# Spilled attention outputs kept as one fp32 piece in three device tensors, and a place of its own for each token tile's probabilities

## The chip, the cores and the metric

The kernel runs on one core of one Trainium2 chip. The metric is the device time of one execution in microseconds (us); lower is better. Each kernel is timed in several runs and its median counts. One execution of each was also taken by the hardware profiler, which records when each instruction ran, what it waited for and what the DMA queues moved. Engines are called as in the profile: PE is TensorE's multiplier, PEld its loading of weights, DVE is VectorE, ACT is ScalarE, POOL is GpSimd, SP is SyncE, which here only issues DMAs. L12 is line 12 of the kernel.

## What is computed

One decoder layer in fp32 for 512 tokens of width 2048: RMSNorm, an attention mixer with sixteen heads in four groups, a residual add, RMSNorm, a SwiGLU feed-forward block of width 5632, and a last RMSNorm. The mixer has three branches: compressed keys, selected blocks and a sliding window, each with its softmax and its gate. Cut to what matters here:

```python
proj = h @ w_in
q, kc, vc, ks, vs, kw, vw, gl = jnp.split(proj, bounds, axis=-1)
...
p_c = masked_softmax(s_c, mask_c)
o_c = jnp.einsum('bghtc,bcgd->btghd', p_c.astype(vcc.dtype), vcc)
...
o = (gates[:, :, 0, :, :, None] * o_c + gates[:, :, 1, :, :, None] * o_s
     + gates[:, :, 2, :, :, None] * o_w)
return o.reshape(Bsz, S, N_HEADS * DH) @ w_out
```

With 512 tokens every block is selected and the window reaches back over all tokens, so both large branches are causal attention, with keys and values of their own.

## The kernel before, in words

**Numbers.** Every fp32 operand of a product is kept as two fp32r parts, a high one (an ACT copy) and a low one (a DVE subtraction of that copy from the operand). `three` (L267 to L269) multiplies high by high, high by low and low by high, so each product is three matrix multiplications. A weight granule is loaded by DMA into a `raw` tile (L81), split by ACT into `whi` (L97) and by DVE into `wlo` (L98); `take` and `ahead` keep the loads and splits some granules ahead of use. In the attention stage `W.queue` is POOL's queue, elsewhere SP's.

**The attention stage** (L630 to L900) issues all instructions in an order written out by hand, with two interleaved streams. No engine reorders its own instructions.

The first stream is the heads. For head h and token tile t (128 tokens each):

- `scores` (L769) multiplies queries by keys into PSUM (`s`), adds the bias on DVE (L791) and takes the exponential on ACT (L793) into `P[t]`. For the three branches the widths differ with t, so `P[t]` has 4 x 96, 160, 224 or 288 columns for t of 0 to 3.
- `finish` (L796) scales by gate and sum (L798 to L805), transposes in blocks of 32 x 32 on DVE (L806) and stores `P[t]` with four DMAs on SP to `d_p` (L808).
- `fetch` (L810) brings `d_p` back on SP, rearranged, into `PT` (`ptr`, L812).
- `turn` (L819) splits one piece of `PT` into `pth` (ACT, L829) and `ptl` (DVE, L833); for the compressed branch the low part lies in spare rows of `pth` (L831). There are three `pth` and two `ptl`.
- `values` (L836) multiplies the values by it into PSUM (`o`; the compressed branch is L844).
- `head_out` (L849) takes the head's output away.

Only two tiles hold probabilities: `P[0]` and `P[2]` share one, `P[1]` and `P[3]` the other.

A head takes twelve steps. In step i the loop does `turn` number i (nine of them), `values` number i - 2 (so the last in step 10, with `head_out`), and `scores` of the next head in steps 2, 5, 8 and 11 with its `finish` in steps 3, 6, 9 and the next head's step 0. The returns of tiles 1 and 0 are issued in steps 0 and 3, those of tiles 3 and 2 for the next head in step 8.

The second stream, `dense`, fills PE between these steps: projections of queries, keys and values for later heads (`qpair`, `kpair`, `vpair`), and at the end four times `partial`, which multiplies the outputs of heads 0 to 11 by a quarter's columns of the output projection and adds the residual. `pump` closes each step: it runs pieces of `dense` until a goal is reached that grows by 20800 units a head up to 13 heads and by 18300 after. A piece counts 650 units and has three multiplications 512 wide in the projections of queries and keys, and six multiplications 256 wide in `vpair` and `partial`. The whole stream has 13 x 20800 + 4 x 15600 = 332800 units. What is left at the end is run after the last head (`drain_to(100)`).

**The spill.** The normalized input lies in `hn_h` and `hn_l` (16 chunks of 128 rows) until the last projection, `qpair(14)`, has used it; `partial` and the stage after it want the heads' outputs in the same place. So for heads 0 to 11 `head_out` splits the output into two parts and stores both to `d_o` on SP; for heads 12 to 15 it splits straight into `hn_h` and `hn_l`. In `qpair(14)`, after each of its first three granules, `reload_o` brings four heads back with two DMAs of 1 MB on SP.

`partial` loads the residual into a `stage` tile on SP (L702), adds the products (L717) and stores the sum to `d_h` on SP (L718). There is one `stage` tile.

Of the kernel before, what the change touches and what calls it, by code (L numbers as in the profile page):

```python
# [10 lines left out]
F32 = mybir.dt.float32  # L11
F32R = mybir.dt.float32r  # L12
I32 = mybir.dt.int32
AF = mybir.ActivationFunctionType
OP = mybir.AluOpType
# [4 lines left out]
S, D, H, DH, G, HPG = 512, 2048, 16, 128, 4, 4  # L20
NT, KC = S // 128, D // 128
# [152 lines left out]
def nsa_block(ctx: ExitStack, tc: tile.TileContext, x, rel_bias, mix_g, ffn_g, fin_g, w_in, w_out,  # L174
              pos_k, w1k, w2k, pos_v, w1v, w2v, f_in, f_out, onehot, out):
    nc = tc.nc
    mm, act, dve, pool = nc.tensor.matmul, nc.scalar.activation, nc.vector, nc.gpsimd
# [6 lines left out]
    dram = ctx.enter_context(tc.tile_pool(name="dram", bufs=1, space=DRAM))  # L184
# [10 lines left out]
    hn_h, hn_l = hn_t = [hnp.tile([128, KC, S], F32R, name=f"hn_{x}") for x in "hl"]  # L195
    d_t = dram.tile([H, UL], F32, name="d_t")
    d_u = dram.tile([128, H * UL], F32, name="d_u")
    d_c = dram.tile([H, 16 * CL], F32, name="d_c")
    d_o = dram.tile([12, 2, 128, S], F32, name="d_o")
    d_h = dram.tile([S, 256 * N_SPILL], F32, name="d_h")  # L200
    d_r = dram.tile([NT, 128, D], F32, name="d_r")
    d_a = dram.tile([NF // 2, 128, 2 * S], F32, name="d_a")
# [87 lines left out]
    def split_from(psum_ap, hi, lo, scale=None):  # L290
        if scale is None:
            act(hi, psum_ap, AF.Copy)
            dve.tensor_tensor(lo, psum_ap, hi.bitcast(F32), op=OP.subtract)
        else:
            act(hi, psum_ap, AF.Copy, scale=scale)
            dve.scalar_tensor_tensor(lo, psum_ap, scale, hi.bitcast(F32), op0=OP.mult, op1=OP.subtract)
# [53 lines left out]
    with ExitStack() as st1:  # L350
# [11 lines left out]
        with ExitStack() as st0:  # L362
# [79 lines left out]
            p = bank([128, 512])  # L442
            for i in range(N_WARM):
                nc.tensor.transpose(p[:, 128 * (i % 4):128 * (i % 4 + 1)], ident, ident)
            p = bank([128, KC])
# [10 lines left out]
            for q in range(4):  # L456
# [22 lines left out]
                if q == 3:  # L479
                    p = bank([128, S])  # L480
# [100 lines left out]
        for i in range(8):  # L581
# [10 lines left out]
            if i == 1:  # L592
                p = ps1.tile([128, 128], F32, name="tr")
# [27 lines left out]
        p = ps1.tile([96, G, 128], F32, name="tr")  # L621
# [8 lines left out]
    with ExitStack() as st2:  # L630
        ap_ = st2.enter_context(tc.tile_pool(name="ap", bufs=2))
        ps2 = st2.enter_context(tc.tile_pool(name="ps2", bufs=2, space=PSUM))
        kv_tiles(ap_, 1, bufs=1)
        runs = [32 * (2 * t + 3) for t in range(NT)]
        two = [ap_.tile([128, 4 * runs[t]], F32, name=f"p{t}", bufs=1) for t in (2, 3)]
        P = [two[t % 2][:, :4 * runs[t]].rearrange("p (j r) -> p j r", j=4) for t in range(NT)]
        CX = [ap_.tile([128, 32], F32, name=f"cx{t}", bufs=1) for t in range(NT)]
        PT = ap_.tile([128, 4, PT_STEP * 3 + runs[3]], F32, name="ptr", bufs=1)
        d_p = [dram.tile([4, 32, 4, runs[t]], F32, name=f"d_p{t}") for t in range(NT)]
        for t in range(2):  # L640
            pool.memset(two[t], 0.0)
        for t in range(NT):
            pool.memset(CX[t], 0.0)
        done = {"n": 0, "ns": 0}

        def stage_tile():
            return ap_.tile([128, 1024], F32, name="stage", bufs=1)
# [7 lines left out]
        def qpair(h0):  # L655
            ps = proj2()
            end = q_out(ps, h0)
            for i in range(4):
                yield from ws(ps, i, W.take(), end=end)
                if h0 == H - 2 and i < 3:  # L660
                    reload_o(i)
            done["n"] += 1
            yield None

# [27 lines left out]
            yield None  # L692

        def reload_o(i):
            for part, t in enumerate((hn_h, hn_l)):
                nc.sync.dma_start(t[:, 4 * i:4 * i + 4].bitcast(F32),
                                  d_o[4 * i:4 * i + 4, part].rearrange("h p s -> p h s"))

        def partial(cb):
            st = stage_tile().rearrange("p (t c) -> p t c", t=NT)  # L700
            c = slice(256 * cb, 256 * (cb + 1))
            nc.sync.dma_start(st, x[:, c].rearrange("(t p) c -> p t c", p=128))  # L702
            ps = [p.rearrange("p (t c) -> p t c", t=2) for p in proj2()]
            for i in range(3):
                w = W.take()
                for t in range(NT):
                    if i == 2 and t == 2:
                        W.ahead(3)
                    for k in range(4):
                        h = 4 * i + k  # L710
                        three(ps[t // 2][:, t % 2], hn_h[:, h, tok(t)], hn_l[:, h, tok(t)], w[0][:, k], w[1][:, k],
                              h == 0 and t % 2 == 0, h == 11)
                        if k % 2:
                            yield 650
                    if i == 2 and t % 2:
                        b = t // 2
                        dve.tensor_tensor(st[:, 2 * b:2 * b + 2], st[:, 2 * b:2 * b + 2], ps[b], op=OP.add)  # L717
            nc.sync.dma_start(d_h[:, c].rearrange("(t p) c -> p t c", p=128), st)  # L718
            done["n"] += 1
            yield None  # L720

# [13 lines left out]

        def pump(h, step):
            at = h + (step + 4) / STEPS
            goal = 20800 * min(at, 13) + 18300 * max(at - 13, 0)
            while done["ns"] < goal:
                c = next(stream, "end")  # L740
                if c == "end":
                    return
                done["ns"] += c or 0
# [66 lines left out]
        def fetch(t):  # L810

            nc.sync.dma_start(PT[:, :, PT_STEP * t:PT_STEP * t + runs[t]], d_p[t].rearrange("j a i r -> (j a) i r"))  # L812
# [6 lines left out]
        def turn(h, b, kt):  # L819
            n = S - 128 * kt  # L820
            th = ap_.tile([128, 512], F32R, name="pth", bufs=3)
            tl = ap_.tile([128, 512], F32R, name="ptl")
            rows = 128 if b >= 0 else 96
            if b < 0:
                src = arrived(rows, 64, 0, PT_STEP + 64)
            else:
                src = arrived(rows, PT_STEP * kt + 32 * (kt + 1) * b + 32 * kt, kt, PT_STEP + 32 * b)
            th4, tl4 = (x[:rows, :n].rearrange("p (t i s) -> p t i s", i=4, s=32) for x in (th, tl))
            act(th4, src, AF.Copy)  # L829
            if b < 0:  # L830
                dve.tensor_tensor(th4[32:64], src[32:64], th4[32:64].bitcast(F32), op=OP.subtract)  # L831
            else:
                dve.tensor_tensor(tl4, src, th4.bitcast(F32), op=OP.subtract)  # L833
            HS[h]["t", b, kt] = th[:rows, :n], tl[:rows, :n]

        def values(h, b, kt):  # L836
            s, g = HS[h], h // HPG
            first = "o" not in s
            if first:
                s["o"] = ps2.tile([128, 512], F32, name="o", bufs=1)  # L840
            th, tl = s.pop(("t", b, kt))
            o = s["o"][:, 128 * kt:]
            if b < 0:
                mm(o, vcc[:, g], th, start=first, stop=True, skip_group_check=True)  # L844
            else:
                vh, vl = (v[:, kt, 128 * b:128 * (b + 1)] for v in VV[g % 2])
                three(o, vh, vl, th, tl, first, False)

        def head_out(h):  # L849
            o = HS[h]["o"]  # L850
            if h < 12:
                f = [ap_.tile([128, S], F32R, name=f"of{i}", bufs=1) for i in range(2)]
                split_from(o, *f)
                for i in range(2):
                    nc.sync.dma_start(d_o[h, i], f[i].bitcast(F32))
            else:
                split_from(o, hn_h[:, h], hn_l[:, h])
            del HS[h]
# [3 lines left out]
        load_bias(1)  # L862
        for i in range(4):
            scores(0, 3 - i)
            if i:
                finish(0, 4 - i)
            if i > 1:
                fetch(5 - i)
            pump(-1, min(9 + i, 11.7))
        for h in range(H):  # L870
            seq = [(b, kt) for kt in (3, 2, 1, 0) for b in (0, 1)] + [(-1, 0)]
            for i in range(STEPS):
                if i == 4:
                    load_bias(h + 2)
                if i in (0, 3):
                    fetch(1 - i // 3)
                if i < 9:
                    turn(h, *seq[i])
                if i == 8 and h + 1 < H:
                    fetch(3)  # L880
                    fetch(2)
                if i == 0:
                    finish(h, 0)
                if h + 1 < H:
                    if i == 2:
                        drain_to(needed(h + 1))
                    if i % 3 == 2:
                        scores(h + 1, 3 - i // 3)
                    elif i % 3 == 0 and i:
                        finish(h + 1, 4 - i // 3)  # L890
                if 2 <= i < 11:
                    if i == 2 and h % HPG == 0:
                        drain_to(h)
                    values(h, *seq[i - 2])
                    if i == 10:
                        head_out(h)
                pump(h, i)
        W.queue = nc.sync
# [78 lines left out]
    hn_h, hn_l = n2_hl  # L977
# [512 lines left out]
```

## Time and profile before

| | us |
|---|---|
| median of 3 runs | 2137.48 |
| lowest and highest | 2137.11 and 2138.2 |
| the profiled execution | 2137.68 |
| its span, first to last instruction | 2136.0 |
| PE busy in the span | 2103.2 |
| DVE, ACT, POOL busy | 1634.8, 922.9, 118.2 |

The span is some 1.7 us shorter than the time of the profiled execution. In a row by stretches stand the stretch, its length, and then for each engine the time busy and the number of instructions in parentheses; at its end stand the granted TensorE clock as a share of full speed, the share of time that the DMA engines were busy, and GB/s. A row of a timeline has the start, the duration, engine, line, operation and tiles; brackets hold the idle time of that engine just before, and what ended it. A row of waits has the waiting engine and line, what it waited for, the total, how often, and the longest. In a group of instructions stand the busy time and the mean duration in ns.

### The profile page before, as it was taken

To read this page: it belongs to the slowest core of one execution; us is meant where nothing else is said; L and a number is where in the kernel's file an instruction comes from. 1 tells how busy PE (TensorE), PEld (TensorE's weight loads), DVE (VectorE), ACT (ScalarE), POOL (GpSimd) and SP (SyncE) were. 2 spreads that over 40 slices of the span, in tenths; PEclk is the share of its full clock that TensorE was granted. 3 is DMA by queue.
4 is the path that set the end of the run, shared out by engine and by line. 5 is a ranking of instruction groups with operands and counts; after the bars stand their busy time and mean duration, and the time that the engine had idled before them with its cause. 6 is when DMAs were issued, how large, how long until landed. Compare 5 with 4: busy or idle time off the path is not lost.

```text
span 2136.0 us, 37198 instructions
## 1 busy us (share of the span) xinstructions
PE 2103.2 (98%) x14697; PEld 1949.5 (91%) x14697; DVE 1634.8 (77%) x2680; ACT 922.9 (43%) x1433; POOL 118.2 (6%) x195
## 2 busy tenths in 40 slices
PE   9999999999998999999999999999999999999998
PEld 7898788898988889899999999999999888999996
DVE  5565777878776357898888888888888787877785
ACT  5344454555544234444444343443434444544344
POOL 1000111111100000000000000000000000001000
PEclk9999999999999999999999999999999999999999
DMA  7555777776787643344434344433344776878894
GB/s 226 174 158 149 195 203 202 194 209 197 207 295 211 218 137 111 118 130 128 129 126 122 122 126 129 129 119 125 123 129 129 256 278 220 299 268 308 307 336 143
DMA packets 279147, 394.37 MB, mean 185 GB/s; under 512 B 34763, under 2 KB 208891, under 8 KB 278332
## 3 DMA queue, kind: packets, MB, share of 16 engines
q1 hardware_dynamic: 255324, 289.68, 43.5%
q0 software_dynamic: 21744, 98.12, 13.3%
q10 hardware_dynamic: 1904, 4.20, 0.5%
q8 instruction: 115, 1.88, 0.4%
q14 instruction: 60, 0.49, 0.1%
HBM read 323.67 MB, written 73.50 MB: 186 GB/s over the span
## 4 chain that ended last, share of the span: by engine, by line
PE 87%; DVE 5%; DMA 4%; ACT 2%; issue 2%; SPq 1%; POOL 0%; ACTq 0%; DVEq 0%; POOLq 0%
PE f L268 19%; PE f L269 19%; PE f L267 19%; PE proj L267 7%; PE proj L268 6%; PE proj L269 6%; DMA d_p<-p 1%; DVE wlo L98 1%; DMA ptr<-d_p 1%; PE pp L269 1%; PE pp L268 1%; PE pp L267 1%; PE po L269 1%; PE po L267 1%; PE po L268 1%
## 5 line engine op out<-in xcount | busy, mean ns | idle before, releaser
L98 DVE TENSOR_TENSOR wlo<-raw,whi 128x1024 fp32r<-128x1024 f32 (+1 forms) x226 | 270.6, 1200 | 117.2 <-ACT whi L97 116.7
L97 ACT ACTIVATE whi<-raw 128x1024 fp32r<-128x1024 f32 (+1 forms) x226 | 234.4, 1040 | 230.4 <-DVE raw L989 124.7
L989 DVE TENSOR_TENSOR tlo<-tt,thi 128x1536 fp32r<-128x1536 f32 (+2 forms) x135 | 197.1, 1460 | 110.1 <-ACT thi L1091 89.1
L267 PE MATMUL f<-hn_h,whi 128*128 128x256 f32 x984 | 271.7, 276 | 0.8 <-ACT E L1049 0.8
L269 PE MATMUL f<-hn_h,wlo 128*128 128x256 f32 x984 | 271.6, 276 | 0.0
L268 PE MATMUL f<-hn_l,whi 128*128 128x256 f32 x984 | 271.6, 276 | 0.0
L1086 ACT ACTIVATE whi<-raw 128x1024 fp32r<-128x1024 f32 x123 | 126.1, 1057 | 292.2 <-DVE raw L989 281.9
L267 PE MATMUL proj<-hn_h,whi 128*128 128x512 f32 x512 | 204.1, 399 | 0.5 <-ACT hn_h L402 0.5
L268 PE MATMUL proj<-hn_l,whi 128*128 128x512 f32 x512 | 200.7, 392 | 0.3 <-DVE hn_l L403 0.3
L269 PE MATMUL proj<-hn_h,wlo 128*128 128x512 f32 x512 | 200.9, 392 | 0.0
L267 PEld LDWEIGHTS f<-hn_h,whi 128*128 128x128 f32 x984 | 184.7, 188 | 1.2 <-ACT E L1049 1.2
L269 PEld LDWEIGHTS f<-hn_h,wlo 128*128 128x128 f32 x984 | 184.7, 188 | 0.0
L268 PEld LDWEIGHTS f<-hn_l,whi 128*128 128x128 f32 x984 | 184.7, 188 | 0.0
L1091 ACT ACTIVATE thi<-tt 128x1536 fp32r<-128x1536 f32 x82 | 121.8, 1486 | 84.8 <-PE f L268 75.3
L989 DVE TENSOR_TENSOR wlo<-raw,whi 128x1024 fp32r<-128x1024 f32 x123 | 147.0, 1223 | 0.0
L267 PE MATMUL proj<-whi,hn_h 128*128 128x256 f32 (+2 forms) x496 | 146.7, 296 | 0.0
L269 PE MATMUL proj<-whi,hn_l 128*128 128x256 f32 (+2 forms) x496 | 146.0, 294 | 0.0
L268 PE MATMUL proj<-wlo,hn_h 128*128 128x256 f32 (+2 forms) x496 | 145.9, 294 | 0.0
L269 PE MATMUL f<-whi,tlo 128*128 128x512 f32 x320 | 124.9, 390 | 0.6 <-DVE tlo L989 0.6
L268 PE MATMUL f<-wlo,thi 128*128 128x512 f32 x320 | 125.0, 391 | 0.0
L267 PE MATMUL f<-whi,thi 128*128 128x512 f32 x320 | 124.7, 390 | 0.0
L269 PEld LDWEIGHTS proj<-hn_h,wlo 128*128 128x128 f32 x512 | 96.5, 189 | 21.5 <-DVE wlo L98 0.2
(323 smaller groups left out, 6087.1 us busy)
## 6 DMA issues: line engine op xcount, KB each, us to landing
raw<-in_ffn_w_in SPq DMA_DIRECT2D x135, 512.0 KB, 3.8
raw<-in_ffn_w_out SPq DMA_DIRECT2D x88, 512.0 KB, 5.7
rawx<-in_ffn_w_in SPq DMA_DIRECT2D x41, 512.0 KB, 4.8
rawx<-d_a SPq DMA_DIRECT2D x31, 512.0 KB, 5.2
ah<-d_s POOLq DMA_DIRECT2D x16, 896.0 KB, 7.0
al<-d_s POOLq DMA_DIRECT2D x16, 896.0 KB, 9.5
raw<-in_nsa_w_in SPq DMA_DIRECT2D x24, 512.0 KB, 5.1
raw<-in_nsa_w_in POOLq DMA_DIRECT2D x24, 512.0 KB, 4.7
```

The source lines that it names most:

```text
L97: self.nc.scalar.activation(hi[:, :n], src, AF.Copy)
L98: self.nc.vector.tensor_tensor(lo[:, :n], src, hi[:, :n].bitcast(F32), op=OP.subtract)
L267: mm(o, ah, bh, start=start, stop=False, skip_group_check=True)
L268: mm(o, ah, bl, start=False, stop=False, skip_group_check=True)
L269: mm(o, al, bh, start=False, stop=stop, skip_group_check=True)
L989: dve.tensor_tensor(o, a, b, op=OP.subtract)
L1086: act(h, r, AF.Copy)
L1091: act(h, ttf, AF.Copy)
```

## The change

- `d_o` becomes three tensors of four heads, with one fp32 piece for each head instead of two parts.
- `head_out` of heads 0 to 11 copies the output by ACT into the `stage` tile and stores that, with one DMA.
- `reload_o` brings four heads back into `hn_l` alone, with one DMA of 1 MB on POOL's queue.
- A new `split_o` splits two heads in place: ACT copies from `hn_l` to `hn_h`, DVE subtracts. Two such splits are issued in `qpair(14)`, after its third and its last granule, and four in the first `partial`, ahead of the pieces of tiles 0 and 2 of its granules 0 and 1.
- `partial` loads `stage` and stores to `d_h` on POOL's queue, and the load comes after its second granule is taken.
- `P[t]` has a tile for each t; POOL clears all four, largest first.
- Before head 0 the return `fetch` goes ahead of the next tile's `finish`.
- The goal of `pump` grows by 22500 units a head after 13 heads, not by 18300.
- `turn` of the compressed branch takes no `ptl` tile.
- The last of the nine `values`, and `head_out`, move from step 10 to step 11.

```diff
-    d_o = dram.tile([12, 2, 128, S], F32, name="d_o")
+    d_o = [dram.tile([4, 128, S], F32, name=f"d_o{i}") for i in range(3)]
...
-        two = [ap_.tile([128, 4 * runs[t]], F32, name=f"p{t}", bufs=1) for t in (2, 3)]
-        P = [two[t % 2][:, :4 * runs[t]].rearrange("p (j r) -> p j r", j=4) for t in range(NT)]
+        P = [ap_.tile([128, 4, runs[t]], F32, name=f"p{t}", bufs=1) for t in range(NT)]
...
-        for t in range(2):
-            pool.memset(two[t], 0.0)
-        for t in range(NT):
+        for t in reversed(range(NT)):
             pool.memset(CX[t], 0.0)
+            pool.memset(P[t], 0.0)
...
                 yield from ws(ps, i, W.take(), end=end)
                 if h0 == H - 2 and i < 3:
                     reload_o(i)
+                if h0 == H - 2 and i > 1:
+                    split_o(i - 2)
...
         def reload_o(i):
-            for part, t in enumerate((hn_h, hn_l)):
-                nc.sync.dma_start(t[:, 4 * i:4 * i + 4].bitcast(F32),
-                                  d_o[4 * i:4 * i + 4, part].rearrange("h p s -> p h s"))
+            pool.dma_start(hn_l[:, 4 * i:4 * i + 4].bitcast(F32), d_o[i].rearrange("h p s -> p h s"))
+
+        def split_o(k):
+            h, l = (x[:, 2 * k:2 * k + 2] for x in (hn_h, hn_l))
+            act(h, l.bitcast(F32), AF.Copy)
+            dve.tensor_tensor(l, l.bitcast(F32), h.bitcast(F32), op=OP.subtract)
...
-            nc.sync.dma_start(st, x[:, c].rearrange("(t p) c -> p t c", p=128))
             ps = [p.rearrange("p (t c) -> p t c", t=2) for p in proj2()]
             for i in range(3):
                 w = W.take()
+                if i == 1:
+                    pool.dma_start(st, x[:, c].rearrange("(t p) c -> p t c", p=128))
                 for t in range(NT):
+                    if not cb and i < 2 and t % 2 == 0:
+                        split_o(2 + 2 * i + t // 2)
...
-            nc.sync.dma_start(d_h[:, c].rearrange("(t p) c -> p t c", p=128), st)
+            pool.dma_start(d_h[:, c].rearrange("(t p) c -> p t c", p=128), st)
...
-            goal = 20800 * min(at, 13) + 18300 * max(at - 13, 0)
+            goal = 20800 * min(at, 13) + 22500 * max(at - 13, 0)
...
-            tl = ap_.tile([128, 512], F32R, name="ptl")
+            tl = ap_.tile([128, 512], F32R, name="ptl") if b >= 0 else th
...
             if h < 12:
-                f = [ap_.tile([128, S], F32R, name=f"of{i}", bufs=1) for i in range(2)]
-                split_from(o, *f)
-                for i in range(2):
-                    nc.sync.dma_start(d_o[h, i], f[i].bitcast(F32))
+                f = stage_tile()[:, :S]
+                act(f, o, AF.Copy)
+                nc.sync.dma_start(d_o[h // 4][h % 4], f)
...
             scores(0, 3 - i)
+            if i > 1:
+                fetch(5 - i)
             if i:
                 finish(0, 4 - i)
-            if i > 1:
-                fetch(5 - i)
...
-                if 2 <= i < 11:
+                if 2 <= i < 10 or i == 11:
                     if i == 2 and h % HPG == 0:
                         drain_to(h)
-                    values(h, *seq[i - 2])
-                    if i == 10:
+                    values(h, *seq[min(i - 2, 8)])
+                    if i == 11:
                         head_out(h)
```

## The prediction

> **What bounds the kernel now.** I read the page first, then the busy time by stretches, then TensorE's (PE's) own waits, and last the order of each engine's work around the places where PE stands. The page:
>
> ```profile
> span 2136.0 us, 37198 instructions
> ...
> PE 2103.2 (98%) x14697; PEld 1949.5 (91%) x14697; DVE 1634.8 (77%) x2680; ACT 922.9 (43%) x1433; POOL 118.2 (6%) x195
> ```
>
> PE is busy 2103.2 of 2136.0 us: no change off PE's path can win more than 33 us, and only by closing its gaps. The stretches (PE busy comes second, PEclk third from the end) show where those are:
>
> ```profile
> 200.00:240.00 40.00, 33.23 (x152) 26.62 (x151) 28.08 (x86) 18.09 (x50) 3.00 (x4) 0.96 0.61 166
> 240.00:580.00 340.00, 338.21 (x1927) 296.29 (x1926) 270.34 (x744) 172.99 (x461) 49.27 (x66) 1.00 0.71 201
> 604.00:621.00 17.00, 12.94 (x96) 11.82 (x95) 9.87 (x31) 7.08 (x20) 1.50 (x2) 0.99 1.06 386
> 621.00:664.00 43.00, 39.62 (x298) 37.62 (x298) 32.65 (x90) 18.77 (x51) 4.51 (x6) 0.97 0.65 196
> 664.00:711.00 47.00, 44.85 (x335) 42.88 (x334) 25.71 (x59) 17.75 (x40) 3.55 (x5) 0.96 0.61 184
> 620.60:624.00 3.40, 3.40 (x18) 3.40 (x18) 3.35 (x10) 1.13 (x5) 0.59 (x1) 0.51 0.41 116
> 692.20:695.60 3.40, 3.40 (x17) 3.40 (x17) 1.29 (x2) 2.01 (x4) 0.00 (x0) 0.50 0.62 201
> ```
>
> The reader is to see three things. Attention starts with 6.8 us idle (40.00 less 33.23). Heads 1 to 11 lose only 1.8 us in 340. From 604 to 711, where head 12 ends and the spilled outputs return, 9.6 us are idle (4.06, 3.38, 2.15); and after two of those gaps the granted clock is half for 3.4 us, about 1.7 us lost each time. PE's waits from 580 on, and then from 240 to 580:
>
> ```profile
> PE o L267 <- ACT pth L829: 5.6, 3, 2.7
> PE o L268 <- DVE ptl L833: 2.3, 1, 2.3
> PE o L844 <- DVE pth L831: 1.3, 1, 1.3
> ```
> ```profile
> PE o L844 <- DVE pth L831: 1.3, 4, 0.4
> ```
>
> All of it, 9.2 us late and 1.3 us earlier, is `values` waiting for `turn`: PE outruns the softmax, return and split of its operand. Two of the late waits come early in that stretch:
>
> ```profile
> 605.18 0.28 PE L267 MATMUL proj<-whi,hn_h 128*128 128x256 f32 x1
> ...
> 607.18 0.28 PE L269 MATMUL proj<-whi,hn_l 128*128 128x256 f32 x1
> 608.79 0.50 PE L844 MATMUL o<-pth,vcc 96*128 96x512 f32 x1 [1.33 <-DVE pth L831]
> ...
> 620.01 0.33 PE L267 MATMUL o<-pth,v1h 128*128 128x128 f32 x1 [2.73 <-ACT pth L829]
> ```
>
> They are 1.33 and 2.73 us; the other three of the late waits make 9.2 - 4.06 = 5.1 us. At 605.18 PE begins `partial(0)`, and its lines follow each other every 0.118 us (2.00 us over 17 gaps).
>
> **The change part by part.**
>
> *The first heads.* P[0] and P[1] no longer share a place with P[2] and P[3], and `fetch` goes ahead of the next tile's stores.
>
> ```profile
> 216.62 0.51 ACT L793 ACTIVATE p<-u,mx 128x256 f32<-128x256 f32 x1 [3.64 <-DMA d_p<-p]
> ```
> ```profile
> 217.59 0.61 SPq L812 DMA_DIRECT2D ptr<-d_p  x1
> ```
> ```profile
> 222.32 0.30 PE L267 MATMUL o<-pth,v0h 128*128 128x128 f32 x1 [2.51 <-issue]
> ```
>
> ACT's 3.64 us for the place go. But PE's 2.51 us hang on the return issued at 217.59. The store it needs had landed by 216.6, since that landing released ACT; so the return can go about 1 us earlier. Behind it on SP stand the next tile's four stores, and behind them its return: those come later by the issue of 0.6 us and the wait ahead of it, and a later value waits for them. I take 0.6 us of gain; bounds 2.5 (the whole wait) and -0.5.
>
> *The last value of each head* moves from step 10 to step 11, a step of some 2 us more for DVE's line L831: the 1.3 us of 240:580 go. Bounds 0 and 2.3 (lines stretched, not counted as idle). The 1.33 us at 608.79 goes too; it is counted below. Leaving `tl` out removes no instruction.
>
> *The spill.* Per head below 12 one DVE line, one store and one split less; six ACT and six DVE lines of double width more, all at heads 12 and 13.
>
> ```profile
> L293 DVE TENSOR_TENSOR of<-o,of x12: 652/653/692, 251.0 to 582.4; 128x512 fp32r<-128x512 f32 x12
> ```
> ```profile
> L98 DVE TENSOR_TENSOR wlo<-raw,whi 128x1024 fp32r<-128x1024 f32 x218 | 264.4, 1215 | 114.6 <-ACT whi L97 114.1 <-DMA x<-in_x 0.2
> L97 ACT ACTIVATE whi<-raw 128x1024 fp32r<-128x1024 f32 x218 | 228.8, 1052 | 225.7 <-DVE raw L989 124.7 <-PE proj L268 22.9 <-PE po L269 15.5
> ```
>
> DVE loses 12 x 0.65 = 7.8 us where PE idles next to nothing, worth nothing there, and gains 6 x 1.2 = 7.3 us (ACT 6 x 1.05 = 6.3) where it does. **The wait that this adds is the main term.** `split_o(1)` stands at the end of `qpair(14)`, so it is issued in the pump of head 12's step 9, behind `q_out` and behind `finish(13, 1)`. `partial(0)` uses head 2 after six lines. On DVE this is what stands ahead:
>
> ```profile
> 609.57 0.69 DVE L319 SCALAR_TENSOR_TENSOR yt<-proj,ybc 128x512 f32<-128x512 f32 x1
> ...
> 612.86 0.84 DVE L806 STREAM_TRANSPOSE p<-p 128x640 f32<-128x640 f32 x1
> ```
>
> PE would reach head 2 at 605.18 + 6 x 0.118 = 605.9. DVE does the second head of `q_out` at 609.57 and ends `finish` at 612.86 + 0.84 = 613.7. Its chain is perhaps 0.6 us earlier without head 11's split and up to 1 us earlier with a quicker return, and 1.2 us later by `split_o(0)`: 613.2. Then 1.2 us for the subtraction: 614.4. PE waits **8.3 us** (allowing 0.2 for the lines that need only the ACT part). Behind it on PE stand the rest of `partial`, head 13's last scores and all values, and ACT and DVE soon wait for those scores; nothing covers it. Bounds: 11 (both splits, nothing earlier) and 0 (DVE in time after all). Half clock after it: one window, 1.7 us; bounds 0 and 3.4. The other four splits run while PE works on: head 13's chain starts afresh after this wait.
>
> [...]
>
> *The returns* are three of 1 MB on POOL instead of six on SP:
>
> ```profile
> hn_h<-d_o SPq DMA_DIRECT2D x3, 1024.0 KB, 8.7
> hn_l<-d_o SPq DMA_DIRECT2D x3, 1024.0 KB, 10.1
> ```
> ```profile
> raw<-in_nsa_w_in SPq DMA_DIRECT2D x24, 512.0 KB, 5.1
> raw<-in_nsa_w_in POOLq DMA_DIRECT2D x24, 512.0 KB, 4.7
> ```
>
> The DMA share of 1.06 over 604:621 with 386 GB/s is their six megabytes. With half of them the probabilities come back sooner; and PE is 4 us and more later anyway. So the 1.33 and 2.73 us vanish. POOL holds each return until PE has read `hn_l`; behind it stand weight loads, which wait for a later granule themselves. The same weights land in 4.7 us from POOL and 5.1 from SP, so I charge the queue nothing (bounds 0 and 3 us).
>
> *Stage and d_h on POOL.*
>
> ```profile
> 640.55 0.39 SPq L718 DMA_DIRECT2D d_h<-stage  x1
> 643.69 0.39 SPq L702 DMA_DIRECT2D stage<-in_x  x1
> 644.18 1.59 SPq L812 DMA_DIRECT2D ptr<-d_p  x2
> ```
>
> SP issues `partial`'s store at 640.55, stands at the load of `stage`, which waits for it, until 643.69, and has the two returns behind it. That hold-up of some 3 us goes, to POOL, where only weight loads stand behind it.
>
> *The pump goal.* A head from 13 on takes 22500 instead of 18300 units, 650 for six lines: 6 x 0.118 / 650 x 4200 = 4.6 us more filler a head, so PE asks later for each value. With SP free this covers the other 5.1 us and the second half-clock window. The price: the stream of 332800 units now ends at head 13 + 62400 / 22500 = 15.77, in step 5 of head 15; the last five values stand bare.
>
> ```profile
> 674.30 0.29 PE L267 MATMUL s<-k1h,qh 128*128 128x288 f32 x1
> ```
> ```profile
> 690.63 0.52 SPq L812 DMA_DIRECT2D ptr<-d_p  x1
> ```
> ```profile
> 693.59 1.15 ACT L829 ACTIVATE pth<-ptr 128x512 fp32r<-128x512 f32 x2 [2.84 <-PE proj L269]
> ```
>
> The last return is issued 16.3 us after head 15's last scores and is in use 19.3 us after. PE gets there after seven steps of three pieces (18 lines x 0.118 = 2.1 us) and four values of some 0.4 us (an estimate from their three lines): 16.5 us. As late as before, the return would cost 2.8 us and a turn's lines on ACT and DVE, 4.1 in all; unhindered on SP only the turn's, 0.5. I take 1.5, nearer to the second, since the hold-up goes.
>
> **Sum**: -0.6 (start) - 1.3 (last values) + 8.3 (split) + 1.7 (its window) - 9.2 (late waits) - 3.4 (two windows) + 1.5 (bare end) = -3.0 us. The profiled execution took 2137.68 us (span 2136.0 and 1.7 around it): 2134.7. The median is 2137.48, 0.2 less; I take **2134.6**.
>
> **The rivals.** 0.2%, 4.3 us, is what a measurement here tells from no change: faster is below 2133.2, slower above 2141.8.
>
> *DVE is in time* (no wait at head 2). For it: DVE is relieved of 0.65 us a head. Against: its line at 609.57 is for work that PE had done by 605.18, and `finish` stands behind it by order. Price: 8.3 + 1.7 back, 2124.6.
>
> *Softmax stays the bound* of heads 13 to 15, the slower side. Place: the chain of scores, `finish`, store, return and `turn`. It decides where a head's chain takes longer than PE's work on it, 24.5 us of filler (34.6 pieces of 6 x 0.118) and the head's own scores and values. For it: before, values wait three times after 621, and 7.3 us of DVE and 6.3 of ACT are added at heads 12 and 13; against: 240:580, with as much filler, hardly waits. Then the 5.1 us and the 1.7 of a window stay, and the bare end costs 4.1 instead of 1.5: 2134.6 + 9.4 = 2144.0.
>
> *The returns come late* from POOL (the change then doesn't free what it means to). ACT would stand at `split_o(0)` with head 12's turns behind it. Price, if 3 us late: 2137.6. Against it: 4.7 beside 5.1 us above. [...]
>
> **How the numbers follow.** Forecast 0.55, with a range of its own of 2131 to 2139, 0.20 of the chance below 2133.2. In time 0.17; softmax-bound 0.17; late returns 0.11. Faster 0.20 + 0.17 = 0.37; same 0.35 + 0.11 = 0.46; slower 0.17. Signs are mixed, so the range runs from 2125 to 2143, leaving out about half of each outer case.
>
> **What would show it.** A wait of PE of some 8 us in front of a `proj` line, put down to `hn_l`, near 606 to 614, and half clock after it; no wait L844; no waits for `ptr` in heads 13 and 14; head 15's last values back to back with gaps below 1 us. Wrong, if PE has no such wait, if `o` lines still wait after 630, or if the stretch before 240 moves by more than 2.5 us.

## The result and the profile after

The changed kernel takes **2144.95 us** (median of 11 runs, 2141.34 to 2147.56) against 2136.86 us for the kernel before (11 runs, 2135.3 to 2141.5): a ratio of 1.0034, 95% interval 1.0025 to 1.0043. It is slower by a third of a per cent, where 2134.6 was forecast. The profiled execution took 2143.05 us, 8.4 us more than the 2134.7 forecast for it and 5.4 more than the profiled execution before.

Its span is 2141.3 us. Its busy time by the same stretches as before (PE busy second, PEclk third from the end), and then one stretch more of the kernel before:

```profile
200.00:240.00 40.00, 34.15 (x152) 27.94 (x151) 26.46 (x83) 18.14 (x50) 3.05 (x5) 0.91 0.59 166
240.00:580.00 340.00, 339.66 (x1934) 297.48 (x1934) 265.56 (x736) 172.47 (x461) 49.24 (x66) 1.00 0.68 193
580.00:604.00 24.00, 21.38 (x92) 17.59 (x91) 12.70 (x41) 9.64 (x28) 3.74 (x5) 0.86 0.91 288
604.00:621.00 17.00, 7.31 (x35) 5.61 (x34) 14.01 (x29) 9.94 (x17) 1.50 (x2) 0.80 0.52 164
621.00:664.00 43.00, 42.29 (x329) 41.41 (x330) 31.85 (x84) 20.21 (x52) 6.00 (x8) 0.96 0.58 172
664.00:711.00 47.00, 45.50 (x364) 43.92 (x363) 31.64 (x78) 19.34 (x46) 8.04 (x11) 1.00 0.71 217
```
```profile
580.00:604.00 24.00, 24.00 (x122) 20.43 (x121) 18.14 (x52) 11.65 (x31) 1.50 (x2) 1.00 0.95 316
```

Up to 580 the changed kernel is ahead, and behind 621 it idles less than before (2.2 us instead of 5.5). All that is lost is lost between 580 and 621: PE idles 2.62 us in 580 to 604, where before it idled not at all, and 9.7 us in 604 to 621 instead of 4.1. PE's waits there, one by one:

```profile
597.54 0.69 PE L267 MATMUL o<-pth,v1h 128*128 128x384 f32 x1 [2.62 <-ACT pth L835]
611.04 0.50 PE L268 MATMUL o<-ptl,v1h 128*128 128x512 f32 x1 [1.97 <-DVE ptl L839]
618.39 0.58 PE L267 MATMUL proj<-whi,hn_h 128*128 128x256 f32 x1 [5.91 <-ACT hn_h L699]
621.28 0.58 PE L269 MATMUL proj<-whi,hn_l 128*128 128x256 f32 x1 [2.10 <-DVE hn_l L700]
```

The last two are the wait for `split_o(1)`: 5.91 + 2.10 = 8.0 us, forecast 8.3. But it ends at 621.28, not at the forecast 614.4, since the first two, which were not forecast, came ahead of it. They are head 12's values waiting for `turn`, and `turn` waits for the probabilities' return. ACT's row shows the first (a second wait of ACT for `ptr`, 3.90 us, ends at 604.37), and below it stands the half clock that followed (6.00 us with PE busy in 5.96 of them):

```profile
596.96 0.94 ACT L835 ACTIVATE pth<-ptr 128x384 fp32r<-128x384 f32 x2 [6.22 <-DMA ptr<-d_p]
```
```profile
597.50:603.50 6.00, 5.96 (x15) 4.80 (x16) 2.09 (x8) 2.12 (x7) 0.00 (x0) 0.50 0.99 309
```

What the queues did, before (SP alone) and after (SP, then POOL):

```profile
581.06 2.81 SPq L808 DMA_DIRECT2D d_p<-p  x4
583.92 0.92 SPq L855 DMA_DIRECT2D d_o<-of  x2
586.23 0.53 SPq L812 DMA_DIRECT2D ptr<-d_p  x1
586.88 1.98 SPq L808 DMA_DIRECT2D d_p<-p  x4
588.90 0.43 SPq L696 DMA_DIRECT2D hn_h<-d_o  x1
589.37 0.54 SPq L696 DMA_DIRECT2D hn_l<-d_o  x1
592.98 0.54 SPq L812 DMA_DIRECT2D ptr<-d_p  x1
```
```profile
580.32 3.69 SPq L814 DMA_DIRECT2D d_p<-p  x4
584.05 0.44 SPq L860 DMA_DIRECT2D d_o<-stage  x1
589.22 0.53 SPq L818 DMA_DIRECT2D ptr<-d_p  x1
589.84 2.92 SPq L814 DMA_DIRECT2D d_p<-p  x4
597.70 0.52 SPq L818 DMA_DIRECT2D ptr<-d_p  x1
```
```profile
580.20 0.75 POOL L695 DMA_DIRECT2D hn_l<-d_o  x1 [3.35 <-PE proj L268]
```

The reader is to see the moment of the first return. On SP it stood, by SP's own order, behind tile 1's stores, the return of tile 1 and tile 0's stores, and went at 588.90. On POOL only PE's last use of `hn_l` holds it, and it goes at 580.20, 0.12 us ahead of tile 1's stores. Their landing releases the return of tile 1: it is issued 2.4 us after the last store before (583.87 to 586.23) and 5.2 us after it now (584.01 to 589.22). Tile 0's return, which needs its own stores, goes from 592.98 to 597.70.

### The profile page after: what moved, and what is told of

Read it like the earlier page. It is cut to its first block, busy times and chain, and to the rows that moved or that the text cites. A ratio compares the mean times of both kernels' runs of the same rounds, so it can differ in the third digit from the quotient of the medians.

```text
span 2141.3 us, 37148 instructions
## 1 busy us (share of the span) xinstructions
PE 2105.8 (98%) x14697; PEld 1951.4 (91%) x14697; DVE 1634.8 (76%) x2674; ACT 929.2 (43%) x1439; POOL 128.0 (6%) x209
## 4 chain that ended last, share of the span: by engine, by line
PE 67%; DMA 1%; DVE 1%; ACT 1%; issue 0%; SPq 0%; ACTq 0%; DVEq 0%
PE f L268 19%; PE f L269 19%; PE f L267 19%; PE proj L267 1%; PE proj L268 1%; PE proj L269 1%; PE pp L267 1%; PE pp L268 1%; PE pp L269 1%; PE po L268 1%; PE po L267 1%; PE po L269 1%; DMA tt<-d_a 0%; PE pp L245 0%; DMA d_p<-p 0%
## 5 line engine op out<-in xcount | busy, mean ns | idle before, releaser
L839 DVE TENSOR_TENSOR ptl<-ptr,pth 128x128 fp32r<-128x128 f32 (+3 forms) x128 | 60.0, 485 | 76.7 <-ACT pth L835 72.9
```

## The experiments

Each ran in five rounds beside the kernel before, and its ratio is to the runs of those rounds; versions are compared by their ratios. The profile gives a second measure: the first multiplication of the output projection (`po`), the first work after the last head. From there to the end every profile of this study has 1424.9 to 1426.5 us, so what one execution wins or loses up to it stands in this one number (710.37 before). But it is one execution: those profiled of e3, e5, e7 and e11 took 2.7 to 4.2 us more than their median, that of the change 1.9 us less. Differences of some 3 us in the last column tell nothing by themselves.

| version | median, us | ratio to before | 95% interval | first `po` |
|---|---|---|---|---|
| the change | 2144.95 | 1.0034 | 1.0025 to 1.0043 | 715.63 |
| e1 returns on SP | 2139.3 | 1.0010 | 1.0001 to 1.0019 | 709.85 |
| e2 early split | 2139.02 | 1.0018 | 1.0008 to 1.0028 | 711.08 |
| e3 both | 2133.38 | 0.9986 | 0.9977 to 0.9994 | 708.62 |
| e4 short returns | 2135.26 | 0.9999 | 0.9991 to 1.0008 | 708.70 |
| e5 returns on POOL, later, early split | 2132.72 | 0.9976 | 0.9968 to 0.9985 | 708.62 |
| e6 e3 with goal 18300 | 2135.47 | 0.9991 | 0.9982 to 1.0000 | 708.59 |
| e7 e3 with the old start | 2131.89 | 0.9974 | 0.9964 to 0.9985 | 707.14 |
| e8 before, last value in step 11 | 2139.99 | 1.0012 | 1.0003 to 1.0020 | 712.43 |
| e9 e5, last value in step 10 | 2131.97 | 0.9976 | 0.9967 to 0.9986 | 703.84 |
| e10 e5 with goal 20400 | 2130.79 | 0.9976 | 0.9966 to 0.9986 | 703.63 |
| e11 e5, subtractions on POOL | 2139.67 | 1.0021 | 1.0009 to 1.0033 | 716.14 |
| e12 e9 and e10 together | 2132.99 | 0.9985 | 0.9972 to 0.9998 | 706.24 |

My theory after the comparison: two costs that add, the returns' collision with head 12's probabilities and the place of `split_o(1)`. The rival: head 12 is late by the new order of the heads' steps, whatever carries the returns.

**e1: the returns on SP.**

```diff
-            pool.dma_start(hn_l[:, 4 * i:4 * i + 4].bitcast(F32), d_o[i]...
+            nc.sync.dma_start(hn_l[:, 4 * i:4 * i + 4].bitcast(F32), d_o[i]...
```

> The changed kernel with its three returns of spilled outputs issued by SP again, not by GpSimd; all else as changed. Theory (the returns, issued up to 8.7 us earlier from GpSimd's queue, run beside head 12's probability stores and returns and make these late): the two waits of ACT for ptr in head 12 (6.22 and 3.90 us) shrink below 2 us each, PE's 2.62 us for pth and 1.97 us for ptl at 597 to 611 and the half clock of 596 to 605 go; the 8 us for hn_h and hn_l stays and begins earlier; 5 to 8 us less than the changed kernel, about 2138. Rival (head 12 is late because of the new order of last value, fetch and splits, whatever queue the returns have): PE's waits in head 12 stay, within 2 us of the changed kernel, about 2144.

Measured: 0.24% less than the change, some 5 us. PE's waits from 580 to 725:

```profile
PE proj L267 <- ACT hn_h L699: 5.9, 1, 5.9
PE proj L269 <- DVE hn_l L700: 2.1, 1, 2.1
PE o L268 <- DVE ptl L839: 1.4, 4, 0.5
PE o L267 <- ACT pth L835: 1.1, 1, 1.1
```
```profile
614.00 0.58 PE L269 MATMUL proj<-whi,hn_l 128*128 128x256 f32 x1 [2.10 <-DVE hn_l L700]
```

The 2.62 us are gone, the 1.97 us have shrunk to 0.50, and ACT's two waits for `ptr` (6.22 and 3.90 us) are gone too; the 8.0 us are untouched and end at 614.00 instead of 621.28. So the collision cost 7.3 us up to that point: 4.1 us of waits and some 3 us of half clock (half of 5.96). The theory holds, the rival falls.

**e2: `split_o(1)` right behind `split_o(0)`.** Both need only the first return.

```diff
-                if h0 == H - 2 and i > 1:
-                    split_o(i - 2)
+                if h0 == H - 2 and i == 2:
+                    split_o(0)
+                    split_o(1)
```

> The changed kernel with split_o(1) issued right behind split_o(0), one step of qpair(14) earlier, ahead of q_out and finish on ACT and DVE. Theory (split_o(1) stands too late by order): the waits for hn_h and hn_l in partial(0) (5.91 and 2.10 us) fall below 1 us together and the half clock after 618 goes, 7 to 10 us less than the changed kernel, about 2136. Rival (the place of the split doesn't matter since head 12's chain is late anyway, and PE then waits for head 12's values or head 13's instead): PE's idle time between 580 and 664 falls by less than 3 us and the time by less than 3 us, about 2143.

Measured: 0.16% less than the change, 3.4 us, between the two expectations; the two intervals overlap a little, so the size is rough. The 5.91 us are gone:

```profile
PE o L267 <- ACT pth L836: 3.6, 2, 3.4
PE proj L269 <- DVE hn_l L701: 2.6, 1, 2.6
```

Of the 8.0 us for the returned outputs 2.6 are left: `partial` now meets the next unready split. The collision is still there; its first wait is 3.43 us instead of 2.62, but it ends at 598.61, before either split runs (ACT's begin at 604.76), so the splits did not lengthen it.

**e3: both edits.**

> Both edits of the two kernels ahead of it: returns on SP, and split_o(1) right behind split_o(0). If the two costs are separate and add, 12 to 17 us less than the changed kernel, 2128 to 2133, and faster than the kernel before. If one hides behind the other, no more than the better of the two alone: 2136 to 2138.

Measured: 0.48% less than the change, 10.3 us, where 0.24 and 0.16 make 0.40. By the ratios the costs add. The `po` column does not show it: 7.0 us won by both edits, 5.8 and 4.6 by each alone. But the profiled execution of e3 was 2.7 us above its median, so the question stays open there. This version is 0.14% faster than the kernel before.

**e4: the returns cut to an eighth.** Each return brings 64 of the 512 tokens, so most of the spilled outputs' part of the output projection is left out.

```diff
-  hn_l[:, 4 * i:4 * i + 4].bitcast(F32), d_o[i].rearrange("h p s -> p h s")
+  hn_l[:, 4 * i:4 * i + 4, :64].bitcast(F32), d_o[i][:, :, :64].rearrange("h p s -> p h s")
```

> The changed kernel with every return cut to its first 64 of 512 tokens, an eighth of the bytes, on the same queue at the same place; the other tokens of the spilled outputs are not brought back, so their part of the output projection is left out of the result. Theory (it is the 3 MB of the returns that make head 12's stores and returns late): ACT's 6.22 and 3.90 us for ptr fall below 2 us each, PE's waits of 2.62 and 1.97 us and their half clock go, 5 to 8 us less than the changed kernel. Rival one (it is the order on the queues, not the bytes): ACT's two waits stay within 1 us, time within 2 us of the changed kernel. Rival two (fetch(1) goes 3 us later for a reason of its own, which is SP's order): fetch(1) is still issued near 589, and PE's 2.62 us stay, but the 1.97 us go.

Measured: 0.35% less than the change, 7.5 us, with queue, moment and order unchanged. Tile 1's stores and its return in this kernel:

```profile
581.03 2.83 SPq L814 DMA_DIRECT2D d_p<-p  x4
...
586.42 0.53 SPq L818 DMA_DIRECT2D ptr<-d_p  x1
```

The return goes 2.6 us after the last store again (583.86 to 586.42). So it is the bytes. Rival one falls, and so does rival two: the return is issued early again, so what had made it late was the late landing of the stores. PE's 2.62 us are gone and its 1.97 us are 0.48, while the 8.0 us stand as they were.

**e5: POOL keeps the returns, one piece later.** This parts the queue from the moment; e2 is its other half.

```diff
-                if h0 == H - 2 and i < 3:
-                    reload_o(i)
+                if h0 == H - 2 and i > 0:
+                    reload_o(i - 1)
```

> GpSimd keeps the returns, but each goes one piece of qpair(14) later (reload_o(i - 1) instead of reload_o(i)), about where SP issued them; split_o(1) stands right behind split_o(0), as in e2 and e3. Theory (it is when the returns run that counts, since they then share the DMA engines with head 12's stores and returns): fetch(1) of head 12 is issued near 586 again, ACT's long waits for ptr go, time as in e3, 2132 to 2135 (ratio 0.998 to 0.999). Rival (GpSimd's queue itself is the cost, whatever the moment): as e2, ratio near 1.002, 2138 to 2140, ACT still waits for ptr 4 to 6 us.

Measured: 0.42% less than e2, and no slower than e3. POOL's first return, and the return of tile 1 on SP:

```profile
587.14 0.76 POOL L696 DMA_DIRECT2D hn_l<-d_o  x1
```
```profile
584.74 0.53 SPq L819 DMA_DIRECT2D ptr<-d_p  x1
```

PE's wait for `hn_l` ends at 614.48, in e2 at 622.45. It is the moment, not the queue. e3 and e5 agree: their first returns go at 588.24 from SP and at 587.14 from POOL, and their ratios, 0.9986 and 0.9976, have intervals that overlap.

**e6 and e10: the pump's goal.** On e3 the old 18300, on e5 20400.

```diff
-            goal = 20800 * min(at, 13) + 22500 * max(at - 13, 0)
+            goal = 20800 * min(at, 13) + 18300 * max(at - 13, 0)
```

> e3 with the pump's goal from head 13 on put back from 22500 to 18300. By the forecast's steps (more filler covers 5.1 us of late waits and 1.7 us of half clock, and costs 1.5 us at the end of head 15): 4 to 6 us slower than e3, 2137 to 2139, with PE's waits for pth or ptl at heads 13 and 14 back. Rival (SP's hold-up by the stage load was the cause of those waits, and it has gone to GpSimd, so the filler is not needed): within 1.5 us of e3.

> e5 with the pump's goal from head 13 on at 20400, half way between 18300 and 22500. If the filler only moves the same waits between heads 13 and 14 and the end of head 15 (what e6 beside e3 suggests: idle time of 621 to 664 up by 2.7 us, of 664 to 711 down by 2.4): within 1.5 us of e5, with the idle time between the two. If the waits at both ends shrink faster than filler moves: 2 to 3 us faster than e5, near 2130.

The stretches 621 to 664 and 664 to 711 of e3 (22500), e6 (18300) and e10 (20400):

```profile
621.00:664.00 43.00, 41.96 (x339) 40.95 (x339) 34.06 (x93) 19.69 (x51) 7.12 (x10) 1.00 0.70 209
664.00:711.00 47.00, 42.77 (x304) 39.66 (x303) 26.77 (x63) 18.13 (x40) 7.29 (x10) 0.96 0.68 210
```
```profile
621.00:664.00 43.00, 39.22 (x296) 37.71 (x295) 34.22 (x91) 19.48 (x52) 6.74 (x9) 0.96 0.69 200
664.00:711.00 47.00, 45.21 (x340) 42.83 (x339) 25.22 (x57) 17.46 (x38) 7.35 (x10) 1.00 0.65 189
```
```profile
621.00:664.00 43.00, 41.52 (x326) 39.88 (x325) 34.18 (x90) 18.65 (x51) 7.50 (x10) 1.00 0.71 211
664.00:711.00 47.00, 46.56 (x335) 43.75 (x334) 24.97 (x58) 18.14 (x40) 7.30 (x10) 1.00 0.72 227
```

With 22500 PE idles 1.0 and 4.2 us, with 18300 3.8 and 1.8, and the lower clock (0.96 in that stretch) goes along; `po` begins at the same time, 708.62 and 708.59. Between these two goals the filler only moves the idle time to the end of head 15. The medians of e3 and e6 differ by 2.1 us and the ratios by 0.05%, with intervals that overlap: no gain of 4 to 6 us from the goal. At 20400 both stretches are good in the profile (1.5 and 0.4 us; e5, with 22500, has 0.5 and 4.2), yet the ratio is e5's: the profiled execution of e5 was the slowest of its runs, that of e10 the fastest, and whether the gain lasts over runs is open.

**e7: the old start.** Ahead of head 0, in e3:

```diff
-            if i > 1:
-                fetch(5 - i)
             if i:
                 finish(0, 4 - i)
+            if i > 1:
+                fetch(5 - i)
```

> e3 with fetch behind finish again ahead of head 0, as before the change; the places of the probabilities stay apart. By the forecast's step: 0.6 us slower than e3 (bounds -0.5 and 2.5); the first value's wait grows by up to 0.6 us and the later wait by 0.5. Rival (the swap gains nothing because the second return goes later by it): first scores of head 1's later steps within 0.2 us of e3, time within 1 us.

Measured: not slower than e3 (0.9974 and 0.9986, overlapping). No gain of the swap shows; 0.6 us would be below what these intervals can tell.

**e8 and e9: the last value's step.** e8 moves it alone, in the kernel before; e9 moves it back in e5 and keeps the rest of the change, the spill in one piece among it.

```diff
-                if 2 <= i < 11:
+                if 2 <= i < 10 or i == 11:
...
-                    values(h, *seq[i - 2])
-                    if i == 10:
+                    values(h, *seq[min(i - 2, 8)])
+                    if i == 11:
```

> The kernel before with only the last value and head_out of every head moved from step 10 to step 11. Forecast's step: the 1.3 us of waits of L844 in 240 to 580 go and the 1.33 us at 608.79 too, 1.3 to 2.6 us less than before, 2134 to 2136. Rival (the waits only move to the next line that needs pth or ptl): PE's busy time in 240 to 580 grows by less than 0.5 us from 338.21, no change of the time.

> e5 with every head's last value and head_out back at step 10, as in the kernel before; the spill in one piece stays. Forecast's step (the move to step 11 by itself takes 1.3 us of waits of L844 away): in 240 to 580 the waits of the vcc line are back, 1 to 2 us slower than e5. Rival (the move only shifts the wait to the scores, whose first lines k0h and k1h lengthened from 291 to some 310 ns, and DVE's 0.65 us a head less is what gained): the vcc line stays near 400 ns without waits, the first score lines fall to 291 ns again, up to 1 us faster than e5.

The lines `s<-k1h`, which belong to the second and the fourth group of heads (heads 4 to 7, and head 12 as far as 575): first and last start, in the kernel before, the change, e8 and e9:

```profile
L267 PE MATMUL s<-k1h,qh x39: 280/291/396, 314.8 to 572.3; 128*128 128x288 f32 x19, 128*128 128x512 f32 x10, 128*128 128x256 f32 x10
```
```profile
L267 PE MATMUL s<-k1h,qh x39: 280/291/402, 314.5 to 570.6; 128*128 128x288 f32 x19, 128*128 128x512 f32 x10, 128*128 128x256 f32 x10
```
```profile
L267 PE MATMUL s<-k1h,qh x39: 280/292/402, 313.9 to 574.0; 128*128 128x288 f32 x19, 128*128 128x512 f32 x10, 128*128 128x256 f32 x10
```
```profile
L267 PE MATMUL s<-k1h,qh x39: 280/291/396, 315.6 to 571.7; 128*128 128x288 f32 x19, 128*128 128x512 f32 x10, 128*128 128x256 f32 x10
```

The same work (1484 lines of PE each) takes 257.5 us before, 256.1 in the change, **260.1** with the move alone and 256.1 with the move undone. The ten versions that share the change's code up to there take 254.8 to 256.4, so single profiles differ by 1.6 us. e8's 2.6 us are more than that, and its ratio, 1.0012, says the same: the move loses by itself. In the changed kernel it neither wins nor loses what could be told. The `vcc` line, to which the forecast looked, before, in e8 and in e9 (240 to 572):

```profile
L844 PE MATMUL o<-pth,vcc 96*128 96x512 f32 x11 | 5.2, 471 | 1.8 <-DVE pth L831 1.3
```
```profile
L844 PE MATMUL o<-pth,vcc 96*128 96x512 f32 x11 | 4.4, 401 | 0.0
```
```profile
L851 PE MATMUL o<-pth,vcc 96*128 96x512 f32 x11 | 5.3, 481 | 1.2 <-DVE pth L838 1.1
```

With the move it loses its wait, and without the move the wait is back; so far the forecast is right. But with the move other lines pay, and e9 has the ratio of e5. The same two lines of a later `values`, before and in e8:

```profile
558.92 0.22 PE L267 MATMUL o<-pth,v0h 128*128 128x128 f32 x1
558.98 0.27 PE L268 MATMUL o<-ptl,v0h 128*128 128x128 f32 x1
```
```profile
560.25 0.22 PE L267 MATMUL o<-pth,v0h 128*128 128x128 f32 x1
560.53 0.33 PE L268 MATMUL o<-ptl,v0h 128*128 128x128 f32 x1
```

The line that needs `ptl` starts 0.28 us after the one ahead of it instead of 0.06, and no idle time is noted: the first line itself lasts 0.22 us in both. Counted from start to start over the whole work, the `vcc` lines and those beside them take 3.1 us less in e8, the `ptl` lines 4.0 more and the first lines of the scores 1.7 more. In the change the same three are 3.1 less, 0.6 and 1.2 more. In e9 the `vcc` lines take 1.4 us less and nothing else changes. What they wait for is DVE, so this fits the DVE line less in each head's spill; that line was not taken out alone, and the tiles' own places and the `turn` without `ptl` changed with it.

**e11: the subtractions of `split_o` on POOL.**

```diff
-            dve.tensor_tensor(l, l.bitcast(F32), h.bitcast(F32), op=OP.subtract)
+            pool.tensor_tensor(l, l.bitcast(F32), h.bitcast(F32), op=OP.subtract)
```

> e5 with the six subtractions of split_o on GpSimd instead of VectorE. If VectorE's 7.3 us of added lines in heads 12 and 13 cause PE's waits for ptl and hn_l there (2.6 us and part of 4.3): these shrink and the time falls by 2 to 4 us, near 2130. If GpSimd's line takes over 4 us: PE waits for hn_l longer than now, 3 to 10 us slower than e5; the trace gives its duration.

```profile
L701 POOL TENSOR_TENSOR hn_l<-hn_l,hn_h 128x1024 fp32r<-128x1024 f32 x6 | 14.1, 2374 | 4.6 <-ACT hn_h L700 4.6
```

Measured: 0.45% slower than e5. The line takes 2374 ns on POOL (1206 on DVE in e5), below the 4 us that I had named, and still PE waits 5.7 us for `hn_l` and 6.2 for `ptl` (2.6 and 4.3 in e5). The second wait I had not thought of. POOL's first two subtractions, a DVE line that began with them, and the same line in e5:

```profile
599.01 4.76 POOL L701 TENSOR_TENSOR hn_l<-hn_l,hn_h 128x1024 fp32r<-128x1024 f32 x2 [2.52 <-ACT hn_h L700]
```
```profile
599.02 2.48 DVE L812 TENSOR_SCALAR p<-cx,sm 128x96 f32<-128x96 f32 x1
```
```profile
597.92 0.28 DVE L812 TENSOR_SCALAR p<-cx,sm 128x96 f32<-128x96 f32 x1
```

DVE's small line lasts 2.48 us instead of 0.28, about as long as one of POOL's (4.76 us for two). That POOL's line held it is my reading of these rows; how was not shown.

**e12: e9 and e10 together.**

> e5 with both e9's edit (last value at step 10) and e10's (goal 20400): the version that the runs point to. Each alone reached the output projection near 704.5 us in its profile instead of 708.6. If these were the same slack at the end of head 15: 2130 to 2132, ratio 0.997 to 0.998. If they add: 2127 to 2129, ratio below 0.997.

Measured: 0.9985, above the ratios of both expectations and not below either alone. They do not add. e5, e7, e9 and e10 stand at 0.9974 to 0.9976 with intervals that cover each other: 5 us faster than the kernel before, and no finer choice between them can be told.

## Why the prediction was wrong

**The step that failed** is that of the returns: "POOL holds each return until PE has read `hn_l` ... so I charge the queue nothing (bounds 0 and 3 us)". I weighed the queue's speed (4.7 against 5.1 us a load) and it was the moment that counted. I read what holds a return on POOL, but not what had held it on SP: the rows at 586.23 to 588.90 were in the trace of before, and they put the return behind head 12's stores and its first return. Freed of that order, 1 MB starts ahead of the stores that PE's next values need. It costs 7.3 us up to 621 (e1: 614.00 against 621.28), 5.8 at `po` (709.85 against 715.63), and by the ratios 5 (e1) to 7.5 us (e4). At `po` the change is 5.3 us behind the kernel before, and the sum had it 3.0 us ahead; of these 8.3 us the two waits and their half clock make 4.6 + 3.0 = 7.6. The rival *The returns come late* named 3 us, and the wrong victim: the late transfer is not the returned output but the probabilities.

A reading behind this step was wrong too. The 386 GB/s of 604 to 621 are not the six megabytes of the returns: the three pairs were issued at 588.90, 596.26 and 604.98, so only the last, 2 MB, starts in that stretch.

**The wait of `split_o(1)`** was right: PE stood 8.0 us for 8.3, and in e1, free of the collision, it ended at 614.00 for 614.4. Its price was oversized: 8.3 + 1.7 = 10 us on paper, by the ratios 3.4 us (e2 against the change) to 5 us (e3 against e1), by the single profiles 4.6 and 1.2. That "nothing covers it" was wrong: without the wait (e3) PE waits 4.6 us for `ptl` and 2.3 for `pth`, with it (e1) 1.4 and 1.1. My reading is that the softmax runs ahead while PE stands; what a wait covers was not measured by itself.

**The window behind it** was forecast at 1.7 us. In e1 the clock was half from 607.6 to 618 with PE busy in 4.79 us:

```profile
607.60:618.00 10.40, 4.79 (x20) 4.50 (x21) 7.75 (x18) 4.80 (x10) 0.73 (x1) 0.54 0.75 245
```

At half clock half of 4.79 is lost, 2.4 us, within the bound of 3.4, an estimate of mine (two windows of 1.7; before, one followed each of two gaps). In the change PE is busy in 4.32 us from 614 to 624.8, at 0.53: 2.0 us.

**The late waits and their windows** (-9.2 and -3.4) went, nearly as forecast: after 630 the change waits 2.1 us in all (0.8 for `pth`, 1.3 for `ptl`; the forecast had named such waits as a sign of being wrong, and 1.5 us for the end of head 15), and no half clock follows (1.00 in 630 to 711). But e6 shows that the larger goal is not always the reason: in a version without the split's wait it wins nothing by the profile, since what it takes from heads 13 and 14 it gives back at the end of head 15. So part of the -12.6 may have been paid by the 8 us wait itself; the change with the old goal was not run. I counted the wait and the gain of the cover that the wait makes as if each stood alone.

**The last values** (-1.3): the size is right, the cause is not. Up to the last `k1h` line the change wins about 1.3 us, but the move alone loses 2.6, and with the move undone the gain is still there. It sits in the `vcc` lines' wait for DVE, and the DVE line less per head, which I valued at nothing, "where PE idles next to nothing", is the likeliest source, not a shown one. PE's idle time was small there, but lines that waited for DVE hid part of it in their overlap, as the rows of e8 show (0.28 us from start to start with no idle time noted).

**The start** (-0.6): the first `k1h` line comes 0.3 us earlier, within the bounds, but it starts at 314.4 to 315.8 in versions with the same start, so nothing can be told, and e7 shows no gain from the order of `fetch`.

**The rivals.** *DVE is in time* fell with the 8.0 us. *Softmax stays the bound* gave 2144.0, near the measured time, but that is luck: by its mechanism heads 13 and 14 wait, and they hardly wait in the change.

## What to carry to other kernels

A queue is also an order. Before a transfer is moved to an idle queue, read from the old queue's rows what it stood behind there; if that was what the critical work needs next, the order was a protection, and the moved transfer needs a place that is as late (one piece of delay gained e5 0.42% against e2). And a wait on the bound engine can be worth less than its length (8.0 us here, worth 3.4 to 5 by the ratios): find the next late thing in a run without it, and price that. Last, one profile is one execution; a gain of a few us in it has to be seen in the runs as well.

## What the runs showed of the hardware

The return of tile 1, which waits for four stores of 80 KB, was issued 2.3 to 3.3 us after the last of them where no return of outputs ran (before, e1, e3, e5), 5.2 us after it where 1 MB had started 0.12 us ahead of the stores (the change), 4.9 in e2, where that transfer has the same place in the program, and 2.6 us after it where it had an eighth of the bytes (e4).

A line of DVE that takes 0.28 us in e5 took 2.48 us in e11, where it began 0.01 us after a subtraction on POOL (two of those took 4.76 us).

SP and ACT kept the order of the program while work behind stood ready. The first return of outputs went from SP at 588.24 in e3, behind its rows of 585.57 and 586.20, and from POOL, where only PE's last use of `hn_l` holds it, at 580.20 in the change. ACT in the change stood 4.20 us, to 611.62, for `yt`, and ran the copy of `split_o(1)`, which stands behind that in the program, from 617.29; in e2, where the copy has its place behind that of `split_o(0)`, both ran from 604.76.

In these runs the length of a wait alone did not tell the half clock after it. A wait of 1.83 us (before, ending at 690.39) was followed by 3.4 us at 0.50, one of 2.62 us (the change) by 6 us at 0.50 with PE busy in 5.96 of them, and one of 2.06 us (e2, ending at 612.02) by none up to 620 (0.98 in 604 to 621). What sets the half clock off was not shown.

Before, two of PE's lines overlapped (the first 0.22 us long, 0.06 us from start to start); in e8 the later of them came 0.28 us after the first, and no idle time was noted. Nor does the busy share show such waits: in 313 to 574 PE was busy in 259.51 us before and in 259.58 in e8, 99% of 261 in both, while the work from the first to the last `k1h` line took 257.5 and 260.1 us.
